# Attention: flipping two query tiles at a time, and taking the values two steps sooner

## The chip, the cores and the metric

One core of one Trainium2 chip. The core has a matrix engine (TensorE, "PE" in the profile, with its weight loads listed apart as "PEld"), a vector engine (DVE), an activation engine (ACT), a general engine (POOL) and a queue that issues transfers (SP). Each works through its own list of instructions in order; they wait for one another through semaphores. The metric is the device time of one execution in microseconds; the figure for a kernel is the median of its runs.

## The reference, cut to what matters

The program is one block of a network on 512 tokens of width 1024: a normalisation, one wide projection, a gated linear attention branch, a softmax attention branch, an output projection and a feed-forward part. The change sits in the softmax attention: 8 heads, 512 keys, the queries taken in four tiles of 128.

```python
def attend(qblk):
    s = jnp.einsum('bhqd,bhkd->bhqk', qblk, kt).astype(jnp.float32)
    p = jax.nn.softmax(s, axis=-1)
    return jnp.einsum('bhqk,bhkv->bhqv', p.astype(vt.dtype), vt)
```

After it come `merged = sigmoid(z_ma) * y_gla + sigmoid(z_mb) * y_mla` and `merged @ w_out`.

## The kernel before

All of it is float32 arithmetic built from three reduced-precision products: a matrix is split into a rounded part ("hi", a copy on ACT) and the remainder ("lo", a subtraction on DVE or POOL), and `mm3` (lines 88 to 90) issues hi·hi, hi·lo and lo·hi. So in the profile one product is three matmuls of the lines L88, L89 and L90, and one split is an ACT instruction of L93 and a DVE or POOL instruction of L94.

The attention is one loop over steps n; a step is one head and one query tile (tile number n = 4·head + query tile, 32 of them). What it issues for a tile:

- `att_scores`: three matmuls (L88 to L90, output `s`, 96 rows by 512 keys), a maximum on DVE (L1071, `top`), the exponential with the row sum on ACT (L1076, `e`).
- `att_normalise`, for two tiles at a time at an even step: a reciprocal on DVE (L1081), the even tile scaled on ACT (L1082), the odd tile scaled on DVE (L1083).
- `att_flip`: the tile's 128x512 probabilities are turned by four transposes on PE (L1091, output `tp`), then split out of PSUM: hi on ACT (L93, `pT`), lo on DVE (L94, `pT`). Two tiles fill the two halves of one pair of buffers `pT`.
- `att_values`, for two tiles: twelve matmuls (`av`, 256 columns, four blocks of keys by three products) that read the whole `pT` pair. L88 reads hi, L89 reads lo. After the second half of a head `merge` multiplies by the gate on DVE (L1119) and adds the other branch on POOL (L1122).

Between them the loop issues other work at fixed steps. At n mod 8 = 2, 3, 4 and 5 a "unit" makes the queries, keys and values of the next two heads (outputs `uq`, `uk`, `uv`: 9, 6, 12 and 12 matmuls) with the splits that belong to them; there are such units for heads 2 to 7, so they stop before step 24. At other steps weights are loaded and split for the output projection, which follows the loop (outputs `wox`, `wow`, `woz`).

In the kernel before, a tile is flipped three steps after its scores (`LAG_B`), one tile a step, and the values of a pair of tiles come six steps after the scores of its second tile (`LAG_C`; pair (0, 1) at n = 7). Written order in a step: normalisation, scores, unit, flip, loads and splits, values.

The written order is not the final one. The framework's planner takes the instructions of the whole program and lays down each engine's list, by priority and by what is ready; PSUM and SBUF buffers are handed out on the way. `s` and `tp` share four PSUM banks (tag "at"), the values and the units the other four (tag "mm"). Two helpers add constraints on the order alone, without a semaphore: `in_program_order` chains the instructions of an engine as written, and `goes_behind(late, early, engines)` puts the first instruction of one range behind the last of another. In the loop before, the maximum and exponential of step n stand behind the splits of the flip of step n - 2; PE's own order is free but for the first steps.

Of the kernel before, what the change touches and what calls it, by code (L numbers as in the profile page):

```python
# [26 lines left out]
MH, NOPE, ROPE, MV = 8, 64, 32, 128  # L27
# [29 lines left out]
def tile_block(ctx: ExitStack, tc: tile.TileContext, t, out: bass.AP):  # L57
# [13 lines left out]
    def u4(name, dt=F32R, shape=(P, 2, S)):  # L71
        return tl(list(shape), dt, "u4", 26, name)
# [4 lines left out]
    def ps(tag, name):  # L77
        serial[0] += 1
        return pp.tile([P, S], F32, tag=tag, bufs=4, name=f"{name}_{serial[0]}")
# [7 lines left out]
    def mm3(acc, lh, ll, rh, rl, start, stop, onto=False):  # L87
        nc.tensor.matmul(acc, lh, rh, start=start, stop=False, skip_group_check=onto)  # L88
        nc.tensor.matmul(acc, lh, rl, start=False, stop=False, skip_group_check=onto)  # L89
        nc.tensor.matmul(acc, ll, rh, start=False, stop=stop, skip_group_check=onto)  # L90

    def split(hi, lo, src, rest=nc.vector):
        nc.scalar.activation(hi, src, AF.Copy)  # L93
        rest.tensor_tensor(lo, src, raw(hi), op=ALU.subtract)  # L94
# [5 lines left out]
    def issued_after(ins, before):  # L100
        tc.add_manual_dep(
            ins, before,
            mybir.DependencyInfo(mybir.DependencyClass.NoSync, mybir.DependencyReason.DATA),
            reason="program order",
        )

    def traced():
        return len(nc.cur_bb.bb.instructions)

    def in_program_order(start, engines=None):  # L110

        prev = {}
        for ins in nc.cur_bb.bb.instructions[start:]:
            if engines is not None and ins.engine not in engines:
                continue
            before = prev.get(ins.engine)
            if before is not None:
                issued_after(ins, before)
            prev[ins.engine] = ins.name

    SP_ONLY = (mybir.EngineType.SP,)
    PE_ONLY = (mybir.EngineType.PE,)
    SPLITTERS = (mybir.EngineType.Activation, mybir.EngineType.DVE)

    def goes_behind(late, early, engines):

        ins = nc.cur_bb.bb.instructions
        for e in engines:
            a, b = [[i for i in ins[x:y] if i.engine == e] for x, y in (early, late)]
            if a and b:  # L130
                issued_after(b[0], a[-1].name)
# [932 lines left out]
    def att_scores(head, qt):  # L1064
        q, kb, _, _ = heads[head]
        tok = slice(qt * P, (qt + 1) * P)
        acc = ps("at", f"s{head}{qt}")
        d = slice(0, NOPE + ROPE)
        mm3(acc, q[d, 0, tok], q[d, 1, tok], kb[d, 0, :], kb[d, 1, :], True, True)
        top = sm("top", 1)  # L1070
        nc.vector.tensor_reduce(top, acc, axis=AX.X, op=ALU.max, negate=True)  # L1071
        e = u2(f"e{head}{qt}")
        if qt % 2 == 0:
            tots[head] = sm("tot", 2)
        tot = tots[head]
        nc.scalar.activation(e, acc, AF.Exp, bias=top, accum_out=tot[:, qt % 2 : qt % 2 + 1])  # L1076
        probs[head, qt] = e

    def att_normalise(head, qt):
        tot, a, b = tots[head], probs[head, qt], probs[head, qt + 1]  # L1080
        nc.vector.reciprocal(tot, tot)  # L1081
        nc.scalar.activation(a, a, AF.Copy, scale=tot[:, 0:1])  # L1082
        nc.vector.tensor_scalar(b, b, tot[:, 1:2], None, op0=ALU.mult)  # L1083

    def att_flip(head, qt):
        e = probs.pop((head, qt))
        if qt % 2 == 0:
            pTs[head, qt // 2] = [u4(f"pT{head}{qt}{x}", F32R, (P, NT, 256)) for x in range(2)]
        tp = ps("at", f"tp{head}{qt}")
        for k in range(NT):  # L1090
            nc.tensor.transpose(tp[:, k * P : (k + 1) * P], e[:, k * P : (k + 1) * P], ident)  # L1091
        hi, lo = pTs[head, qt // 2]
        c = slice((qt % 2) * P, (qt % 2 + 1) * P)
        split(hi[:, :, c], lo[:, :, c], tp.rearrange("p (k q) -> p k q", k=NT))

    def att_values(head, half):
        if half == 0:
            avs[head] = ps("mm", f"av{head}")
        acc = avs[head]
        hi, lo = pTs.pop((head, half))  # L1100
        _, _, vs, c = heads[head]
        for k in range(NT):
            vt = vs[k // 2]
            mm3(acc[:, half * 256 : (half + 1) * 256], vt[:, 0, k % 2, c], vt[:, 1, k % 2, c],
                hi[:, k, :], lo[:, k, :], k == 0, k == NT - 1)
        if head < MH - 1:
            if half == 1:
                merge(head, acc, (0, 1))
        else:
            merge(head, acc, (half,))  # L1110

    def merge(head, acc, halves_):

        p, c = head // 2, slice((head % 2) * HT, (head % 2 + 1) * HT)
        if p not in merged:
            merged[p] = u2(f"mx{p}"), u2(f"my{p}")
        y = g2[head]
        tok = slice(halves_[0] * HT, (halves_[-1] + 1) * HT)
        nc.vector.scalar_tensor_tensor(y[:, tok], y[:, tok], 1.0, acc[:, tok], op0=ALU.add, op1=ALU.mult)  # L1119
        for x in halves_:  # L1120
            t_ = slice(x * HT, (x + 1) * HT)
            nc.gpsimd.tensor_tensor(merged[p][x][:, c], y[:, t_], y1[head][:, t_], op=ALU.add)  # L1122
# [185 lines left out]
    in_program_order(fixed, SPLITTERS)  # L1308
    in_program_order(ordered, PE_ONLY)
    in_program_order(pooled, (mybir.EngineType.Pool,))  # L1310
    LAG_B, LAG_C = 3, 6
    units = up_units(1)
    at = traced()
    next(units)
    goes_behind((at, traced()), first_units, SPLITTERS[:1])
    attending = traced()
    sums_of, flipping, span = {}, {}, {}
    for n in range(4 * MH + LAG_C - 1):
        if n % 2 == 0 and 2 <= n <= 4 * MH:
            att_normalise((n - 2) // 4, (n - 2) % 4)  # L1320
        scored = traced()
        if n < 4 * MH:
            att_scores(n // 4, n % 4)
            if n - 2 in flipping:
                goes_behind((scored, traced()), flipping[n - 2], SPLITTERS)
        scored = scored, traced()
        if n == 0:
            goes_behind(scored, last_gate, PE_ONLY)
        if n == 3:
            span["fourth"] = scored  # L1330
        if 2 <= n % 8 < 7:
            at = traced()
            next(units, None)
            if n == 2:
                gla_turn(GH - 1)
            if n < 4:
                goes_behind((at, traced()), scored, PE_ONLY)
        if n in (6, 14):
            units = up_units(n // 8 + 2)
            at = traced()  # L1340
            next(units)
            if n == 6:
                goes_behind((at, traced()), span["fourth"], SPLITTERS[:1])
        b = n - LAG_B
        if 0 <= b < 4 * MH:
            flips = traced()
            att_flip(b // 4, b % 4)
            flipping[n] = flips, traced()

        if n == 20:  # L1350
            load_onto(B11, B12, w_out)
        extra = traced()
        for x, at in (("y", (18, 26, 34)), ("z", (20, 28, 36))):
            if n in at:
                p = at.index(n)
                to = (5, 6) if x == "y" else (7, 3)
                split_sum(wo_left[p], sums_of[p, x], *to, f"{x}o{p}", nc.gpsimd if p < 2 else nc.vector)
        if n in (19, 30):
            p = (19, 30).index(n)
            split_first(wo_left[p], merged[p][0], f"o{p}", nc.gpsimd)  # L1360
        if n < 4 * MH:
            goes_behind((extra, traced()), scored, SPLITTERS[:1])
        if n == 35:
            split_first(wo_left[2], merged[2][0], "o2")
        if n in (11, 13):
            streamed(1, B11, (n - 11) // 2)
            split_streamed(1, (n - 11) // 2)
        if n in (21, 23):
            streamed(2, B21, (n - 21) // 2)
        if n == 15:  # L1370
            load_w2(0, B11, w_out)
        if n == 17:
            at = traced()
            load_w2(0, B21, w_out, B22)
            span["sums"] = at, traced()
        if n == 23:
            load_onto(B21, B11, w_out)
        if n == 24:
            load_w2(0, B12, w_out)
            load_w2(0, B22, w_out)  # L1380
        c = n - LAG_C
        if c >= 0 and c % 2 == 1:
            att_values(c // 4, (c % 4) // 2)
        if n == 33:
            load_onto(B21, B12, w_out)
        if c > 0 and c % 8 == 7 and c // 8 < NP - 1:
            sums_of[c // 8, "y"], sums_of[c // 8, "z"] = merged_sums(c // 8, nc.gpsimd)
# [345 lines left out]
```

## Time and profile before

| | |
|---|---|
| median of three runs | 757.4 us (757.4 to 757.45) |
| the profiled execution | 757.7 us, of which the span of its instructions is 755.7 us |
| granted PE clock, mean | 0.999 |
| attention, from its first scores to its last values | 297.8 to 381.5 us of the span |
| exponentials, ACT | 32 of 689 ns |
| maxima, DVE | 32 of 682 ns |
| splits of flipped tiles, ACT and DVE | 32 of 597 ns and 32 of 682 ns |
| transposes of the attention, PE | 128 of 274 ns |

A row of a time line gives the start, the duration, the engine, the line, the operation, output <- inputs, shapes and how many instructions were merged; an idle time before the row stands in brackets with what ended it. Durations of matmuls overlap, because each is shown to the end of its pipeline: what a matmul costs in a stream is the distance from its start to the next start. The rows of a table of waits read "who waited <- for whom: us in total, times, longest". In a table of stretches each engine's busy time stands with its number of instructions, then the granted clock, the share of the transfer engines and GB/s.

### The profile page before, as it was taken

To read this page: it belongs to the slowest core of one execution; us is meant where nothing else is said; L and a number is where in the kernel's file an instruction comes from. 1 tells how busy PE (TensorE), PEld (TensorE's weight loads), DVE (VectorE), ACT (ScalarE), POOL (GpSimd) and SP (SyncE) were. 2 spreads that over 40 slices of the span, in tenths; PEclk is the share of its full clock that TensorE was granted. 3 is DMA by queue.
4 is the path that set the end of the run, shared out by engine and by line. 5 is a ranking of instruction groups with operands and counts; after the bars stand their busy time and mean duration, and the time that the engine had idled before them with its cause. 6 is when DMAs were issued, how large, how long until landed. Compare 5 with 4: busy or idle time off the path is not lost.

```text
span 755.7 us, 10257 instructions
## 1 busy us (share of the span) xinstructions
PE 746.8 (99%) x3720; PEld 632.8 (84%) x3720; DVE 586.5 (78%) x850; ACT 461.6 (61%) x780; POOL 165.3 (22%) x238
## 2 busy tenths in 40 slices
PE   9999999999999999999999999999999999999996
PEld 7888888888889888898888988888888888888885
DVE  7777887989787597898897787856696578748795
ACT  8456565686476575988865766345544555345644
POOL 0722110262662632136850100000000000000014
PEclk9999999999999999999999999999999999999999
DMA  9849582611321334228897421461126410650003
GB/s 315 256 125 230 177 174 82 113 29 29 83 57 31 47 86 114 73 84 198 264 201 227 129 57 56 140 194 57 56 65 204 122 57 4 206 153 0 29 1 111
DMA packets 94306, 87.59 MB, mean 116 GB/s; under 512 B 15696, under 2 KB 66896, under 8 KB 94256
## 3 DMA queue, kind: packets, MB, share of 16 engines
q1 hardware_dynamic: 87760, 74.33, 32.8%
q0 software_dynamic: 6208, 12.32, 9.3%
q8 instruction: 29, 0.48, 0.3%
q10 hardware_dynamic: 288, 0.28, 0.1%
q14 instruction: 21, 0.17, 0.1%
HBM read 83.25 MB, written 2.10 MB: 113 GB/s over the span
## 4 chain that ended last, share of the span: by engine, by line
PE 93%; DVE 3%; ACT 2%; DMA 1%; issue 1%; POOL 0%; POOLq 0%; ACTq 0%; SPq 0%
PE f L90 8%; PE f L88 8%; PE f L89 8%; PE gx L88 4%; PE gx L90 4%; PE gx L89 4%; PE first L330 3%; PE gz L90 2%; PE gz L88 2%; PE gz L89 2%; PE zb L88 1%; PE tp L1091 1%; PE zb L90 1%; PE zb L89 1%; PE wox L88 1%; PE wox L90 1%
## 5 line engine op out<-in xcount | busy, mean ns | idle before, releaser
L1672 POOL DMA_DIRECT2D gfin<-in_g_final x1 | 0.6, 628 | 284.1 <-PE f L90 284.1
L961 DVE TENSOR_TENSOR w<-w,w 128x1024 f32<-128x1024 f32 x32 | 38.7, 1221 | 0.3
L1071 DVE TENSOR_REDUCE top<-s 128x1 f32<-128x512 f32 x32 | 21.8, 682 | 2.9 <-PE s L90 2.6
L1076 ACT ACTIVATE e<-s,top 128x512 f32<-128x512 f32 x32 | 22.0, 689 | 2.7 <-DVE top L1071 2.4
L94 DVE TENSOR_TENSOR pT<-tp,pT 128x512 fp32r<-128x512 f32 x32 | 21.6, 682 | 2.4 <-ACT pT L93 2.2
L1399 DVE TENSOR_TENSOR h<-h,gx 128x512 f32<-128x512 f32 x32 | 21.5, 682 | 1.9 <-PE gx L90 1.8
L93 ACT ACTIVATE pT<-tp 128x512 fp32r<-128x512 f32 x32 | 18.9, 597 | 3.2 <-PE tp L1091 3.0
L1091 PE MATMUL tp<-ident,e 128*128 128x128 f32 x128 | 19.3, 274 | 0.4 <-ACT e L1082 0.2
L88 PE MATMUL av<-pT,v 128*128 128x256 f32 x64 | 18.9, 296 | 0.0
L93 ACT ACTIVATE ghb<-y 128x512 fp32r<-128x512 f32 x16 | 10.1, 633 | 14.0 <-DVE y L907 14.0
L1465 ACT ACTIVATE fa<-f 128x512 f32<-128x512 f32 x32 | 18.5, 578 | 0.0
L1091 PEld LDWEIGHTS tp<-ident,e 128*128 128x128 f32 x128 | 15.1, 140 | 3.9 <-ACT e L1082 0.8
L89 PE MATMUL av<-pT,v 128*128 128x256 f32 x64 | 18.2, 285 | 0.0
L90 PE MATMUL av<-pT,v 128*128 128x256 f32 x64 | 18.2, 285 | 0.0
L547 ACT ACTIVATE bds<-bd 128x512 f32<-128x512 f32 x4 | 2.4, 598 | 20.9 <-PE bd L543 20.9
L93 ACT ACTIVATE b_00h<-w 128x1024 fp32r<-128x1024 f32 x7 | 7.4, 1061 | 12.6 <-PE gz L90 6.0
L93 ACT ACTIVATE b_20h<-w 128x1024 fp32r<-128x1024 f32 x7 | 7.4, 1062 | 12.1 <-PE gz L90 6.0
L93 ACT ACTIVATE b_10h<-w 128x1024 fp32r<-128x1024 f32 x7 | 7.4, 1061 | 12.1 <-PE gz L90 6.0
L88 PE MATMUL s<-kbuf,q 96*128 96x512 f32 x32 | 14.2, 444 | 0.1
L1474 ACT ACTIVATE px<-fa 128x256 f32<-128x256 f32 x32 | 13.4, 418 | 1.0
L957 POOL DMA_DIRECT2D w<-in_w_out x10 | 12.3, 1401 | 6.5 <-DVE bo60l L94 5.3
L636 POOL DMA_DIRECT2D gvw<-in_w_in x4 | 4.8, 1226 | 38.7 <-DVE gvw L641 34.0
(1731 smaller groups left out, 2947.8 us busy)
## 6 DMA issues: line engine op xcount, KB each, us to landing
w<-in_w_ff SPq DMA_DIRECT2D x64, 256.0 KB, 3.4
w<-in_w_out POOLq DMA_DIRECT2D x10, 512.0 KB, 8.8
grw<-in_w_in SPq DMA_DIRECT2D x8, 512.0 KB, 9.3
zaw<-in_w_in SPq DMA_DIRECT2D x8, 512.0 KB, 7.9
gvw<-in_w_in SPq DMA_DIRECT2D x8, 512.0 KB, 4.5
w<-in_w_out SPq DMA_DIRECT2D x16, 256.0 KB, 5.9
x<-in_xt SPq DMA_DIRECT2D x8, 256.0 KB, 5.2
vw<-in_w_first SPq DMA_DIRECT2D x8, 256.0 KB, 5.4
```

The costliest lines, as they stand in the source:

```text
L88: nc.tensor.matmul(acc, lh, rh, start=start, stop=False, skip_group_check=onto)
L89: nc.tensor.matmul(acc, lh, rl, start=False, stop=False, skip_group_check=onto)
L90: nc.tensor.matmul(acc, ll, rh, start=False, stop=stop, skip_group_check=onto)
L93: nc.scalar.activation(hi, src, AF.Copy)
L94: rest.tensor_tensor(lo, src, raw(hi), op=ALU.subtract)
L330: nc.tensor.matmul(f_accs[i], a[:, i * P : (i + 1) * P], b, start=k == 0 and x == 0, stop=k == KD - 1 and x == 2)
L961: nc.vector.tensor_tensor(wq[dst][g], wq[x][g], wq[y][g], op=op)
L1071: nc.vector.tensor_reduce(top, acc, axis=AX.X, op=ALU.max, negate=True)
L1076: nc.scalar.activation(e, acc, AF.Exp, bias=top, accum_out=tot[:, qt % 2 : qt % 2 + 1])
L1091: nc.tensor.transpose(tp[:, k * P : (k + 1) * P], e[:, k * P : (k + 1) * P], ident)
L1399: nc.vector.tensor_tensor(hc, hc, acc, op=op)
L1465: nc.scalar.activation(a, acc, AF.Relu)
```

## The change

Three things in the loop. The flips: instead of one tile a step, both tiles of a pair are flipped at the odd step n (tiles n - 3 and n - 2), one directly behind the other, so that the odd tile comes one step sooner; their transposes are chained in written order on PE. The values: `LAG_C` goes from 6 to 4, so that pair (0, 1) is taken at n = 5, two steps after its flip, and `merge` and the sums that hang on it come two steps sooner. The order in an odd step: scores, unit, values of the pair flipped two steps ago, then the two flips; on PE the values stand behind that step's scores, and the flips behind the values. As `flipping` now has entries at odd steps alone, only odd steps have their maximum and exponential held behind the flips of two steps ago. The loop runs as many steps as before (37), and the last half of the last head is still taken after the loop.

```diff
-    LAG_B, LAG_C = 3, 6
+    LAG_B, LAG_C = 3, 4
...
-    for n in range(4 * MH + LAG_C - 1):
+    for n in range(4 * MH + LAG_C + 1):
...
-        b = n - LAG_B
-        if 0 <= b < 4 * MH:
+        c = n - LAG_C
+        if c >= 0 and c % 2 == 1 and c < 4 * MH - 1:
+            valued = traced()
+            att_values(c // 4, (c % 4) // 2)
+            goes_behind((valued, traced()), scored, PE_ONLY)
+        if n % 2 == 1 and LAG_B <= n <= 4 * MH + 1:
             flips = traced()
-            att_flip(b // 4, b % 4)
+            for b in (n - LAG_B, n - LAG_B + 1):
+                att_flip(b // 4, b % 4)
             flipping[n] = flips, traced()
+            in_program_order(flips, PE_ONLY)
+            if c > 0:
+                goes_behind(flipping[n], (valued, flips), PE_ONLY)
...
-        c = n - LAG_C
-        if c >= 0 and c % 2 == 1:
-            att_values(c // 4, (c % 4) // 2)
```

## The prediction, made before the changed kernel ran

> **What bounds the kernel now.** I read the page first, for the engine that sets the end.
>
> ```profile
> span 755.7 us, 10257 instructions
> PE 746.8 (99%) x3720; PEld 632.8 (84%) x3720; DVE 586.5 (78%) x850; ACT 461.6 (61%) x780; POOL 165.3 (22%) x238
> PE 93%; DVE 3%; ACT 2%; DMA 1%; issue 1%; POOL 0%; POOLq 0%; ACTq 0%; SPq 0%
> ```
>
> PE is busy for 99% of the span and is 93% of the chain that ended last. No matmul is added or removed by this change, so it can only act through time in which PE stands still. Next I asked for the waits of PE and of its weight loads within the attention, 296 to 384 us:
>
> ```profile
> PEld tp L1091 <- ACT e L1082: 0.8, 2, 0.7
> PEld tp L1091 <- issue: 0.6, 2, 0.3
> PEld s L88 <- ACT e L1076: 0.3, 1, 0.3
> PE tp L1091 <- ACT e L1082: 0.2, 1, 0.2
> ```
>
> That is all there is to win: 0.8 + 0.6 + 0.3 + 0.2 = 1.9 us. Of it 1.6 us stand before transposes, at two places above all, which the time line of PE shows:
>
> ```profile
> 359.13 0.39 PE L90 MATMUL s<-kbuf,q 96*128 96x512 f32 x1
> 359.75 0.66 PE L1091 MATMUL tp<-ident,e 128*128 128x128 f32 x4 [0.23 <-ACT e L1082]
> ...
> 363.98 0.28 PE L89 MATMUL av<-pT,v 128*128 128x256 f32 x1
> 364.39 0.63 PE L1091 MATMUL tp<-ident,e 128*128 128x128 f32 x4
> ```
>
> Both times the tile was not yet scaled by ACT (L1082). Both lie after step 24, where the units have ended and a pair of tiles has only its own work on PE. There a pair without a wait looks like this:
>
> ```profile
> 365.69 0.40 PE L88 MATMUL s<-kbuf,q 96*128 96x512 f32 x1
> ...
> 366.38 0.60 PE L1091 MATMUL tp<-ident,e 128*128 128x128 f32 x4
> 366.74 0.48 PE L88 MATMUL s<-kbuf,q 96*128 96x512 f32 x1
> ...
> 367.53 0.60 PE L1091 MATMUL tp<-ident,e 128*128 128x128 f32 x4
> 367.88 0.36 PE L88 MATMUL av<-pT,v 128*128 128x256 f32 x1
> 368.09 0.28 PE L89 MATMUL av<-pT,v 128*128 128x256 f32 x1
> ...
> 368.44 0.28 PE L89 MATMUL av<-pT,v 128*128 128x256 f32 x1
> ...
> 369.39 0.40 PE L88 MATMUL s<-kbuf,q 96*128 96x512 f32 x1
> ```
>
> Scores, flip, scores, flip, values: 369.39 - 365.69 = 3.70 us for the pair. Scores cost 366.38 - 365.69 = 0.69. A flip costs 0.44: from its start to the second matmul behind it 368.09 - 367.53 = 0.56, less the 0.12 that a values matmul takes in the stream (three from 368.09 to 368.44). Values cost what is left, 3.70 - 2 x 0.69 - 2 x 0.44 = 1.44.
>
> **The change, part by part: grouping the transposes.** Does a longer run of transposes cost less than two short ones? The kernel already has a run of eight:
>
> ```profile
> 375.43 0.39 PE L89 MATMUL wox<-bo10l,gao 128*128 128x512 f32 x1
> 375.66 1.03 PE L1091 MATMUL tp<-ident,e 128*128 128x128 f32 x8
> 376.45 0.36 PE L89 MATMUL av<-pT,v 128*128 128x256 f32 x1
> 376.65 0.28 PE L90 MATMUL av<-pT,v 128*128 128x256 f32 x1
> ```
>
> By the same reading 376.65 - 375.66 - 0.12 = 0.87, against 2 x 0.44 = 0.88. Sixteen times 0.01 is 0.2 us at most, within the rounding; I take 0. The change has no gain of its own on PE.
>
> A run of eight could also be dearer. The longest run of transposes before is sixteen:
>
> ```profile
> 423.45 1.91 PE L199 MATMUL mb<-ident,ms 128*128 128x128 f32 x16
> 423.00:426.00 3.00, 3.00 (x29) 3.00 (x28) 1.65 (x3) 1.70 (x4) 0.00 (x0) 1.00 0.50 147
> ```
>
> Over it the granted clock stays at 1.00, and it is twice as long as the new runs. [...]
>
> **The wait that goes.** At an odd step the new order on PE is scores, values, flip, flip. Between the last scores of a pair and its first flip PE now does two scores, two flips and two values blocks; before, it did two scores, two flips and one values block. That is 1.44 us more time for the scaling, against waits of 0.7 us at the longest. So I take all 1.6 us before transposes as gone; at the other bound none goes. The 0.3 us that scores waited for a bank stays.
>
> **The wait that comes.** Values of a pair now follow its flips at two steps' distance: flip, flip, scores, scores, values (and the units, where there are any). Before, three scores, three flips and a values block stood there. The splits of both tiles must be done first. What they take:
>
> ```profile
> 354.46 0.60 PE L1091 MATMUL tp<-ident,e 128*128 128x128 f32 x4
> 355.10 0.60 ACT L93 ACTIVATE pT<-tp 128x512 fp32r<-128x512 f32 x1 [0.23 <-PE tp L1091]
> 361.89 0.72 ACT L1082 ACTIVATE e<-e,tot 128x512 f32<-128x512 f32 x1 [0.23 <-DVE tot L1081]
> 362.52 1.08 ACT L93 ACTIVATE pT<-tp 128x512 fp32r<-128x512 f32 x2
> 363.56 1.28 DVE L94 TENSOR_TENSOR pT<-tp,pT 128x512 fp32r<-128x512 f32 x2
> 368.85 0.59 ACT L93 ACTIVATE pT<-tp 128x512 fp32r<-128x512 f32 x1
> 369.47 0.69 DVE L94 TENSOR_TENSOR pT<-tp,pT 128x512 fp32r<-128x512 f32 x1 [0.45 <-ACT pT L93]
> ```
>
> Count from the start of the second flip. ACT can begin a tile 355.10 - 354.46 = 0.64 after its flip started; the first tile's flip started 0.44 earlier, so its hi part starts at 0.20 and ends at 0.80. DVE follows 369.47 - 368.85 - 0.59 = 0.03 later, at 0.83, and two lo parts in a row take 1.28: both are done at 2.11. The second hi part, at 0.20 + 1.08 = 1.28, is not late. PE meanwhile ends the flip at 0.44 and two blocks of scores at 0.44 + 1.38 = 1.82; the first values matmul reads hi and may go, the second, at 1.94, reads lo and waits 0.17. A flip started after a wait is 0.06 longer (0.66 against 0.60), which I take for the refilling of the pipeline. So with ACT and DVE free at the right moment the wait is 0.23 us a pair: the lower bound.
>
> They are not free:
>
> ```profile
> 354.00:365.00 11.00, 10.64 (x73) 9.05 (x72) 10.28 (x20) 9.17 (x20) 8.34 (x10) 1.00 1.07 283
> 365.00:376.00 11.00, 11.00 (x83) 10.10 (x82) 9.47 (x19) 9.48 (x21) 7.60 (x9) 1.00 0.89 257
> ```
>
> (PE, PEld, DVE, ACT, POOL.) ACT is busy 83 to 86% and DVE 86 to 93% of these stretches. The scaling of the next pair by ACT becomes ready at about this moment, since the exponentials of the scores ahead of the values end while the values and flips run. It occupies ACT for 362.52 - 361.89 = 0.63. In front of the hi parts it makes the wait 0.23 + 0.63 = 0.86: the upper bound. Half of it is my value, 0.23 + 0.31 = 0.54, as an engine busy nine tenths of the time is met on average in the middle of an instruction.
>
> Other work can't shorten this within a pair. Values, flip, flip, split, values is now a ring: the flips stand behind the values by order, the values behind the splits by data. One turn is at least 1.44 + 0.88 + the 2.11 - 0.44 = 1.67 that the splits need after the flips, less the 0.12 of the one values matmul that needs no lo, and with 0.06 for the refilling 3.93 us, against 3.70 before. Behind the waiting values matmul stand the two flips and the next scores, and for these DVE's maxima and ACT's exponentials wait.
>
> How many pairs feel it? Where units lie between flip and values there are 1.4 us and more of cover. They don't at n = 7, 9, 15 and 17, nor at n = 23, 25, 27, 29, 31 and 33: ten of the sixteen. At the first four the planner can draw in the next unit, as it does now:
>
> ```profile
> 314.46 0.40 PE L88 MATMUL uq<-cqhl,wq2h 128*128 128x512 f32 x1
> 314.70 0.60 PE L1091 MATMUL tp<-ident,e 128*128 128x128 f32 x4
> 315.05 0.48 PE L89 MATMUL uq<-cqhl,wq2h 128*128 128x512 f32 x1
> ```
>
> I take 0.1 us each there (bounds 0 and 0.86), and the full 0.54 for the six late ones.
>
> **What else moves.** The merge of a head on DVE and POOL comes two steps sooner, and with it the sums for the output projection. On POOL's queue the merge of head 3 now stands ahead of the split of step 19 and that of head 4 ahead of the accumulating load of step 23. POOL has 2.7 us of 11 free in the stretches above, and no wait of PE names POOL, so I take 0; without that room a late load would show as a wait of `wox` or `wow`. On SP's queue nothing changes place. The `pT` buffers are held for two steps instead of four, so no transfer waits longer for one. After the loop PE has no wait listed before 384, and the last values are covered by output products as before: 0.
>
> **The sum.** Six times 0.54 is 3.2, four times 0.1 is 0.4, less 1.6: 2.0 us more. The profiled execution took 757.7 us with a span of 755.7; it would be 759.7, and the median, 0.3 us below it, 759.4. With the lower bound at the six, 6 x 0.23 - 1.6 = -0.2, 757.2; with the upper at all ten, 10 x 0.86 - 1.6 = 7.0, 764.4.
>
> **The rivals.**
>
> *A wash.* Either the splits are served promptly (0.23) and the old waits are merely exchanged for new ones, or the planner, which is bound to keep only values ahead of the two flips, slips the next scores between the two flips and so keeps the old spacing. For it: 0.23 is what free engines give. Against it: ACT and DVE are not free. About 757.2.
>
> *Faster.* The planner fills the six gaps with the first products of the output projection. Twelve of these (four rows by three matmuls), of 375.66 - 375.43 = 0.23 each, 2.8 us, are used now from 375 us on. With gaps of up to 2.8 / 6 = 0.46 us they would all be filled, and 1.6 to 1.9 us of waits vanish: 755.6. For it: the row at 375.43 shows such a product between values and flips. Against it: half of them need the merged pair of heads 2 and 3, the planner did not draw one into the gap at 359, and my gap is above 0.46.
>
> *Every exposed pair waits the full scaling,* in all ten places: 764.4. For it speaks that the planner takes what is ready first, and the scaling is ready first.
>
> *The clock.* If runs of eight transposes lost half the clock, 16 x 0.87 = 14 us: 771.4. [...]
>
> **How the numbers follow.** A measurement of this kernel can tell about 0.2%, 1.5 us, from no change: 755.9 to 758.9 is "same". Forecast (half a scaling in front, slower by 1.5 us or more) 0.50; every pair 0.10; the clock 0.02: slower 0.62. Wash 0.22. Faster 0.16, as 1.9 us is all there is and 1.5 of it would have to be gained net. The range goes from 756.0 to 764.0: it leaves out about 0.08 below, 0.05 of the dear case and the clock. The forecast's own range is 757.2 to 764.4.
>
> **What would show it.** Right: PE's waits in the attention change their name, from transposes waiting for the scaled tile (L1082) to `av` waiting for the lo part (L94, DVE) or the hi part (L93, ACT), most of them after step 22, 0.2 to 0.9 us each; runs of eight transposes cost 0.87. Wrong: no wait of `av` in the late part; scores that stand between the two flips; output products between the values of heads 6 and 7; a wait of `wox` on POOL; a granted clock under 1.00. The forecast fails as a whole if the listed waits of PE between 296 and 384 us sum to less than 2.

## The result, and the profile after

| | before | after |
|---|---|---|
| median | 757.42 us (757.40 to 757.75, 4 runs) | 764.77 us (764.69 to 765.73, 4 runs) |
| ratio | | 1.0097 (95%: 1.0085 to 1.0110) |
| span of the profiled execution | 755.7 us | 762.7 us |
| granted PE clock, mean | 0.999 | 0.998 |

The changed kernel is 7.35 us slower, 7.0 us on the span. The page after has the same matmuls, and the mean clock is the same to 0.001:

```profile
span 762.7 us, 10267 instructions
PE 749.0 (98%) x3720; PEld 632.7 (83%) x3720; DVE 586.5 (77%) x850; ACT 462.3 (61%) x780; POOL 165.3 (22%) x238
PE 91%; issue 3%; DVE 2%; ACT 1%; POOL 1%; DMA 0%; POOLq 0%; SPq 0%; DVEq 0%; ACTq 0%
```

DVE and ACT have hardly more to do than before (586.5 and 461.6 us then). PE stands still for longer, and the waits of its weight loads within the attention say before what:

```profile
PEld av L89 <- DVE pT L94: 6.4, 10, 1.0
PEld s L88 <- ACT e L1076: 2.0, 3, 0.7
PEld av L88 <- ACT pT L93: 1.8, 3, 1.0
PEld tp L1091 <- PE tp L1091: 0.2, 1, 0.2
```

The transposes no longer wait for a scaled tile. The values wait for their split tiles instead, ten times for a lo part, three times for a hi part, and the scores wait for a bank (an `s` that the exponential has not yet read). Weight loads run ahead of matmuls, so part of such a wait costs nothing: the matmuls themselves waited 3.6 us for the lo parts, 1.0 for the hi parts and 0.7 before scores. What it does cost is read from the distance of one pair's flips from the next pair's, on PE's time line of the late part:

```profile
356.14 1.03 PE L1091 MATMUL tp<-ident,e 128*128 128x128 f32 x8
...
360.76 1.26 PE L1091 MATMUL tp<-ident,e 128*128 128x128 f32 x8
...
365.60 1.04 PE L1091 MATMUL tp<-ident,e 128*128 128x128 f32 x8
...
368.26 0.38 PE L88 MATMUL av<-pT,v 128*128 128x256 f32 x1 [0.24 <-ACT pT L93]
...
369.31 0.39 PE L89 MATMUL av<-pT,v 128*128 128x256 f32 x1 [0.67 <-DVE pT L94]
...
370.72 1.04 PE L1091 MATMUL tp<-ident,e 128*128 128x128 f32 x8
...
371.83 0.39 PE L89 MATMUL s<-kbuf,q 96*128 96x512 f32 x1
...
373.96 0.39 PE L89 MATMUL av<-pT,v 128*128 128x256 f32 x1 [0.71 <-DVE pT L94]
...
375.38 1.03 PE L1091 MATMUL tp<-ident,e 128*128 128x128 f32 x8
...
377.33 0.50 PE L88 MATMUL s<-kbuf,q 96*128 96x512 f32 x1 [0.22 <-ACT e L1076]
...
378.58 0.38 PE L89 MATMUL av<-pT,v 128*128 128x256 f32 x1 [0.17 <-DVE pT L94]
...
379.99 1.09 PE L1091 MATMUL tp<-ident,e 128*128 128x128 f32 x8
381.82 0.39 PE L88 MATMUL av<-pT,v 128*128 128x256 f32 x1 [0.74 <-ACT pT L93]
```

Six pairs of flips are shown. A turn, from one of them to the next, holds the two flips, two blocks of scores and one of values, 3.70 us of PE's work. The five turns took 4.62, 4.84, 5.12, 4.66 and 4.61 us: 0.92, 1.14, 1.42, 0.96 and 0.91 too much, 5.35 together. Not all of it stands before values: in the first and the fifth turn about 0.5 stands before scores that waited for a bank (the row at 377.33; the first turn has one like it at 358.09), and 0.44 before the lo part (the row at 378.58). At the sixth place there are no scores left, and the values came 381.82 - 379.99 - 0.87 = 0.96 after the flip's end. That is 6.3 us for the six late places. The old waits of 1.6 us are gone, so the rest of the 7.0 is 7.0 + 1.6 - 6.3 = 2.3 us, in the earlier part. There the same time line has these idle times, one at each of the prediction's four early places (n = 7, 9, 15 and 17):

```profile
314.52 0.38 PE L89 MATMUL av<-pT,v 128*128 128x256 f32 x1 [0.55 <-DVE pT L94]
...
317.89 0.50 PE L88 MATMUL s<-kbuf,q 96*128 96x512 f32 x1 [0.22 <-ACT e L1076]
...
336.83 0.39 PE L89 MATMUL av<-pT,v 128*128 128x256 f32 x1 [0.45 <-DVE pT L94]
...
341.48 0.39 PE L89 MATMUL av<-pT,v 128*128 128x256 f32 x1 [0.24 <-DVE pT L94]
```

They sum to 1.46. An idle time is shown from the end of the last matmul's pipeline, and less than what was lost: at 378.58 it is 0.17, where the lo part's matmul came 0.33 later than it could (its hi part started at 378.13 and takes 0.12 in the stream), and the matmul behind it another 0.1 late. With some 0.2 more for each the four make about 2.3; this is an estimate.

What stood in front of the splits? DVE's time line for the turns from 365.60 and from 370.72:

```profile
367.37 0.69 DVE L1071 TENSOR_REDUCE top<-s 128x1 f32<-128x512 f32 x1 [0.30 <-PE s L90]
367.98 1.28 DVE L94 TENSOR_TENSOR pT<-tp,pT 128x512 fp32r<-128x512 f32 x2
...
370.92 0.69 DVE L1119 SCALAR_TENSOR_TENSOR tb<-tb,av 128x512 f32<-128x512 f32 x1 [1.06 <-PE av L90]
371.52 0.16 DVE L1081 RECIPROCAL tot<-tot 128x2 f32<-128x2 f32 x1
371.78 0.92 DVE L1083 TENSOR_SCALAR e<-e,tot 128x512 f32<-128x512 f32 x1
372.63 1.27 DVE L94 TENSOR_TENSOR pT<-tp,pT 128x512 fp32r<-128x512 f32 x2
```

POOL's, at the scaling of 0.92 us:

```profile
371.68 0.74 POOL L1122 TENSOR_TENSOR mx<-tb,yg 128x256 f32<-128x256 f32 x1 [0.85 <-DVE tot L1081]
```

and ACT's:

```profile
366.51 0.73 ACT L1082 ACTIVATE e<-e,tot 128x512 f32<-128x512 f32 x1 [0.23 <-DVE tot L1081]
367.14 1.07 ACT L93 ACTIVATE pT<-tp 128x512 fp32r<-128x512 f32 x2
...
371.35 1.08 ACT L93 ACTIVATE pT<-tp 128x512 fp32r<-128x512 f32 x2 [0.62 <-PE tp L1091]
```

In the first turn ACT's scaling holds the hi parts back until 367.14, and a maximum, which itself waited 0.30 us for the scores behind the flip, holds the lo parts back until 367.98; the second is done at 369.26 and its matmul starts at 369.31. In the second turn ACT was prompt, but on DVE the merge, the reciprocal and a scaling of 0.92 us (median 0.49 over the kernel) stand in front: the lo parts end at 373.90, the matmul starts at 373.96. The length of this scaling goes with POOL's part of the merge (L1122), which runs beside it: in the whole attention each of the seven scalings that took over 0.5 us ends 0.28 to 0.29 us after an instruction of POOL that runs beside it, here at 372.70 against 372.42. So the merge, which the change brings two steps sooner, stands in front of the lo parts on DVE, and the scaling behind it, beside POOL's part, takes 0.92; at the turn from 360.76 and at the last place it is the same (scalings of 0.92 and 0.98). That POOL's part is what lengthens the scaling is a reading of these rows: no run took that part away. It is not one scaling that is met halfway, but whatever the lists of the two engines hold.

### The profile page after: what moved, and what is told of

It reads as the page before. It is cut to its first block, busy times and chain, and to the rows that moved or that the text cites. A ratio compares the mean times of both kernels' runs of the same rounds, so it can differ in the third digit from the quotient of the medians.

```text
span 762.7 us, 10267 instructions
## 1 busy us (share of the span) xinstructions
PE 749.0 (98%) x3720; PEld 632.7 (83%) x3720; DVE 586.5 (77%) x850; ACT 462.3 (61%) x780; POOL 165.3 (22%) x238
## 4 chain that ended last, share of the span: by engine, by line
PE 91%; issue 3%; DVE 2%; ACT 1%; POOL 1%; DMA 0%; POOLq 0%; SPq 0%; DVEq 0%; ACTq 0%
PE f L89 8%; PE f L88 8%; PE f L90 8%; PE gx L88 4%; PE gx L89 4%; PE gx L90 4%; PE first L330 3%; PE gz L88 2%; PE gz L89 2%; PE gz L90 2%; PE zb L88 1%; PE zb L90 1%; PE zb L89 1%; DVE pT L94 1%; PE av L89 1%
## 5 line engine op out<-in xcount | busy, mean ns | idle before, releaser
L89 PEld LDWEIGHTS av<-pT,v 128*128 128x128 f32 x64 | 12.2, 190 | 6.6 <-DVE pT L94 6.4
L1091 PE MATMUL tp<-ident,e 128*128 128x128 f32 x128 | 16.8, 273 | 0.0
L88 PEld LDWEIGHTS av<-pT,v 128*128 128x128 f32 x64 | 12.1, 190 | 2.3 <-ACT pT L93 1.8
```

## The experiments

Times are compared with runs of the kernel before on the same chip; "+" is the difference of the medians.

| what runs | median, us | + | ratio (95%) |
|---|---|---|---|
| the change (after) | 764.77 | 7.35 | 1.0097 (1.0085 to 1.0110) |
| e1: flips in pairs, values at the old distance | 761.79 | 4.30 | 1.0055 (1.0040 to 1.0070) |
| e2: values two steps sooner, flips single | 761.47 | 3.98 | 1.0051 (1.0034 to 1.0068) |
| e7: values one step sooner, flips single | 759.48 | 1.60 | 1.0024 (1.0014 to 1.0033) |
| e3: after, flips ahead of values | 765.61 | 8.12 | 1.0107 (1.0092 to 1.0122) |
| e4: after, scalings behind the splits | 765.57 | 8.08 | 1.0104 (1.0089 to 1.0119) |
| e17: after, maxima and exponentials behind the splits | 765.90 | 8.10 | 1.0108 (1.0091 to 1.0125) |
| e5: after, no order fixed on PE | 762.38 | 4.50 | 1.0062 (1.0047 to 1.0077) |
| e6: e1, second lo part a step later | 759.97 | 2.09 | 1.0031 (1.0020 to 1.0042) |
| e10: after, second lo part a step later | 767.61 | 9.66 | 1.0132 (1.0118 to 1.0146) |
| e12: after, banks for the late scores | 765.54 | 7.59 | 1.0101 (1.0088 to 1.0115) |
| e11: after, no scalings | 761.88 | 3.93 | 1.0056 (1.0040 to 1.0070) |
| e13: after, no maxima | 762.22 | 4.61 | 1.0054 (1.0039 to 1.0069) |
| e14: after, neither | 765.97 | 8.36 | 1.0107 (1.0092 to 1.0121) |
| e16: e14, exponentials behind the splits | 763.74 | 5.94 | 1.0079 (1.0064 to 1.0094) |
| e9: before, maxima one step behind | 759.00 | 1.12 | 1.0015 (1.0006 to 1.0024) |
| e8: before, flips and values a step later | 759.19 | 1.24 | 1.0024 (1.0015 to 1.0033) |
| e15: e8, the last values one step sooner | 758.08 | 0.47 | 1.0007 (0.9998 to 1.0016) |

### The two halves of the change (e1, e2, e7)

e1 keeps the paired flips and gives the values their old distance:

```diff
-    LAG_B, LAG_C = 3, 4
+    LAG_B, LAG_C = 3, 6
...
-    for n in range(4 * MH + LAG_C + 1):
+    for n in range(4 * MH + 5):
```

> The flips stay paired and chained as in the changed kernel, but the values go back to six steps behind (four steps behind their flips). Theory A (a ring: flips stand behind values on PE, values behind the splits of flips only two steps older, and the splits behind other work on ACT and DVE): the 8.2 us of weight-load waits of av on pT fall under 1 us and the time is 757 to 758.5 us. Rival B (the pairing itself, which makes work for ACT and DVE arrive in bursts, costs the time): the waits stay above 5 us under some name and the time is 762 us or more.

Measured: +4.30. In its waits (weight loads, within the attention) the values are served, and the scores stand instead:

```profile
PEld s L88 <- ACT e L1076: 4.1, 7, 1.0
PEld av L88 <- ACT pT L93: 0.8, 1, 0.8
```

So pairing has a price of its own, which the prediction had at nothing. The reading of these waits is that two splits in a row stand on ACT and DVE, that the maxima and exponentials behind them come later, and the banks of `s` with them; e6 tests it below.

e2 is the other half, the kernel before with the values two steps sooner (the same edit of `LAG_C` in before, the last half still taken after the loop):

```diff
-    LAG_B, LAG_C = 3, 6
+    LAG_B, LAG_C = 3, 4
```

> The kernel before with the values two steps sooner and nothing else: one flip a step, PE's order left to the planner. Theory A: without the order that holds the flips behind the values there is no ring, the planner lays flips and scores into the gap, 757.5 to 760 us. Rival (the shorter distance alone, whatever the order of the flips, costs the time): 763 us or more.

Measured: +3.98, with waits of both kinds:

```profile
PEld av L88 <- ACT pT L93: 1.8, 3, 0.9
PEld tp L1091 <- ACT e L1082: 1.8, 2, 1.3
PEld av L89 <- DVE pT L94: 1.5, 4, 0.5
```

Single flips still wait for their scaling here; only the order "values ahead of flips" of the change removes that. e7 is the same with `LAG_C = 5`:

> The kernel before with the values one step sooner instead of two (757.5 with none, 761.5 us with two). If the distance from split to values decides, with one step (some 1.1 us of scores and a flip) less cover: the waits of av appear in the tight places only, 758 to 760 us. If what costs is the odd step itself, in which values meet scaling and maxima, the values in even steps cost nothing or more than two steps: 757.5 or 762 us.

Measured: +1.60. Six, five and four steps: 0, +1.60, +3.98. Each step that is taken from the distance costs; that the second costs more than the first is not clear of the spread of these runs. Pairing alone (+4.30) and distance alone (+3.98) sum to 8.3, against 7.35 for both.

### The order on PE (e3, e5)

e3 turns the order round: scores, flips, values.

```diff
-            valued = traced()
-            att_values(c // 4, (c % 4) // 2)
-            goes_behind((valued, traced()), scored, PE_ONLY)
...
+            goes_behind(flipping[n], scored, PE_ONLY)
+        if c >= 0 and c % 2 == 1 and c < 4 * MH - 1:
+            valued = traced()
+            att_values(c // 4, (c % 4) // 2)
+            goes_behind((valued, traced()), flipping[n], PE_ONLY)
```

> The changed kernel with the two order constraints exchanged: in each odd step scores, then the two flips, then the values of the older pair. The values get two flips (0.87 us) more of cover and nothing stands behind them in a ring. Theory A: the waits of av, about 1 us each now, shrink to 0.1 to 0.3, and the flips wait for the scaling again by up to 1.6 us in all as before the change: 757.5 to 760 us. Rival C (the maxima, held behind the splits on DVE, starve ACT, whatever the order of flips and values): 762 us or more.

Measured: +8.12. The waits change their name and not their size:

```profile
PEld tp L1091 <- ACT e L1082: 7.6, 5, 2.0
```

With the values behind them the flips meet the unscaled tile again. (This profile is of the longest of the four runs, 767.12 us, in which the clock was 0.50 from 320.4 to 323.8 us; the others took 764.92 to 765.71.) In e5 PE's constraints on flips and values are taken out and the planner chooses:

```diff
-            goes_behind((valued, traced()), scored, PE_ONLY)
...
-            in_program_order(flips, PE_ONLY)
-            if c > 0:
-                goes_behind(flipping[n], (valued, flips), PE_ONLY)
```

> The changed kernel without its new order on PE: the flips no longer stand behind the values nor in a chain, the values no longer behind the scores of their step; distances as in the changed kernel. Theory A (the ring by order): the planner separates flips and values as it can, most of the loss goes, 757.5 to 760 us. Theory D (the distances alone crowd ACT and DVE, whatever the order on PE): 763 to 766 us, and the waits are still those of av on pT and of scores on exponentials.

Measured: +4.50; `av` waits 2.5 + 1.9 us, `s` 1.7, `tp` 0.9. The fixed order is worth 7.35 - 4.50 = 2.85 us of the loss. The rest stays without it; it is the price of the shorter distance and the pairing, which e1 and e2 show each alone.

### Moving work on ACT and DVE (e4, e17)

e4 leaves the scalings in and puts them behind the splits of the last flip:

```diff
+            scaling = traced()
             att_normalise((n - 2) // 4, (n - 2) % 4)
+            if n - 1 in flipping:
+                goes_behind((scaling, traced()), flipping[n - 1], SPLITTERS)
```

> The changed kernel with one constraint more: the reciprocal and the two scalings of a pair stand behind the splits of the flips of the step before, on ACT and on DVE. Theory A with the prediction's term (one scaling in front of the splits): the waits fall towards the bound for free engines, 0.23 us in about ten places, 2 to 3 us in all, and the time is 758.5 to 761 us. Rival C (the maxima and exponentials are late, and the scalings only fill the hole they leave): 763 to 766 us, since the exponentials and what hangs on them are not earlier.

Measured: +8.08, `av` still waits 5.2 + 2.2 us. Its five late turns take 4.02, 5.26, 5.13, 4.03 and 4.63 us, 0.8 less in all than the change's. The clock takes this back: in every run of e4 the mean granted clock was 0.995, and in its profile it was 0.57 over the four us from 316.0, behind 1.5 us in which PE was busy for 0.46. That is as much as 3.4 us at half clock, and loses 1.7 us. Without that spell e4 would be at about +6.4, an estimate: 1 us better than the change, where leaving the scalings out (e11) gains 3.4. e17 does the same with maxima and exponentials:

```diff
+            if n - 1 in flipping:
+                goes_behind((scored, traced()), flipping[n - 1], SPLITTERS)
```

> The changed kernel, whole, with the same constraint: maxima and exponentials of an even step stand behind the splits of the flips of the step before, on DVE and ACT. If maxima that wait for their scores ahead of the splits are a good part of the loss: 761.5 to 763.5 us. If the scalings ahead of the splits and the late exponentials make nearly all of it: 764 to 766 us.

Measured: +8.10:

```profile
PEld av L89 <- DVE pT L94: 6.5, 9, 1.0
PEld s L88 <- ACT e L1076: 2.6, 4, 0.7
PEld av L88 <- ACT pT L93: 2.0, 2, 1.4
```

As measured, neither gains on the change. A likely reason, not shown turn by turn, is that what is put behind the splits of this turn is what the next turn's flips or scores need: the lists must hold it somewhere, and PE asks for it soon.

### The second lo part, a step later (e6, e10)

These take the split of the pair's second tile out of `att_flip` and issue it after the next step's scores, its lo part behind their maximum. e6 does so at the old distance (on e1), e10 at the new one (on after):

```diff
-    def att_flip(head, qt):
+    def att_flip(head, qt, later=False):
...
+        if later:
+            return lambda: split(hi[:, :, c], lo[:, :, c], tp.rearrange("p (k q) -> p k q", k=NT))
...
+        if n - 1 in flipping:
+            at = traced()
+            second()
+            goes_behind((at, traced()), scored, SPLITTERS[1:])
```

> Paired flips with the values at the old distance (the first experiment, 761.8 us, where scores wait 4.1 us for the exponentials that free their bank), but the split of the second tile of a pair is issued behind the next step's scores, its lo part behind their maximum. Theory C (with two splits in a row ahead of it on DVE the maximum comes late, the exponential with it, and the bank): ACT's waits for the maximum fall from 9.4 us towards the 2.4 us of the kernel before, the waits of scores under 2 us, 757.5 to 760 us. Rival (paired transposes cost through something else, such as holding two banks at once): 761 us or more.

> The changed kernel (values two steps sooner, flips paired), with the split of a pair's second tile issued behind the next step's scores and its lo part behind their maximum on DVE. Theory A (the direct ring: flip, split, values): the second lo part comes one maximum, 0.6 us, later and values wait for it, so 0.6 us more in about nine places, 768 to 771 us. Theory C (late maxima and exponentials hold the ring): 760 to 763 us.

Measured: e6 +2.09, half of e1's 4.30; e10 +9.66, 2.3 above after, with these waits:

```profile
PEld av L89 <- DVE pT L94: 9.0, 10, 1.5
PEld av L88 <- ACT pT L93: 4.6, 8, 1.6
```

With distance to spare the split is better behind the maximum, without it worse. It is the same instruction; what decides is which of its neighbours has slack. This is the most direct sign in the runs that in the changed kernel the splits of every pair set PE's pace.

### Banks (e12)

The odd scores of heads 6 and 7 get banks of the other four:

```diff
-        acc = ps("at", f"s{head}{qt}")
+        acc = ps("mm" if head >= 6 and qt % 2 else "at", f"s{head}{qt}")
```

> The changed kernel with the scores of every second tile of heads 6 and 7 in the other four PSUM banks, which the units have left by then. If banks are part of the cost: the two late waits of scores for an exponential (1.3 us with their refilling) go, and scores can run ahead, 760.5 to 763.5 us. If not: 764 to 765.5 us, the waits moving to the values behind them.

Measured: +7.59, no gain; the profiled execution has after's span of 762.7. The late scores do get their banks and run ahead, and the values wait in their place:

```profile
PEld av L89 <- DVE pT L94: 5.2, 9, 0.9
PEld av L88 <- ACT pT L93: 4.3, 6, 1.1
```

The late turns take 4.66, 4.80, 5.11, 4.65 and 4.63 us, within 0.04 of after's, though PE now has nine matmuls of scores to do in the first of them and three in the fifth. So what PE has to do in a turn does not set its length, and neither do the banks: the round from flips through the splits to the values does.

### Leaving work out (e11, e13, e14, e16)

e11 leaves out the two scalings of a pair (L1082, L1083):

```diff
-        nc.scalar.activation(a, a, AF.Copy, scale=tot[:, 0:1])
-        nc.vector.tensor_scalar(b, b, tot[:, 1:2], None, op0=ALU.mult)
```

> The changed kernel with the two scalings of a pair left out (the reciprocal stays, the probabilities go on without their row's factor), which takes 0.63 us from ACT and 0.5 to 0.9 us from DVE per pair, and the link from the exponentials to the flips. Theory D (work crowded into the time between flips and values on ACT and DVE): the waits of av fall from 8.2 to 2 to 3 us, 757.5 to 760.5 us. Theory A in its bare form (the ring is flip, split, values alone, with engines free): no change, 763 to 766 us.

Measured: +3.93, so the scalings are worth 3.4 us of the 7.35. What stays is seen on DVE and on PE at one of its long waits:

```profile
365.47 0.69 DVE L1071 TENSOR_REDUCE top<-s 128x1 f32<-128x512 f32 x1 [0.91 <-PE s L90]
366.08 1.28 DVE L94 TENSOR_TENSOR pT<-tp,pT 128x512 fp32r<-128x512 f32 x2
```

```profile
367.42 0.39 PE L89 MATMUL av<-pT,v 128*128 128x256 f32 x1 [1.18 <-DVE pT L94]
```

DVE stood idle for 0.91 us with the lo parts behind it in its list, because the maximum at the head of the list waited for scores. e13 leaves out the maxima in place of the scalings:

```diff
-        nc.vector.tensor_reduce(top, acc, axis=AX.X, op=ALU.max, negate=True)
...
-        nc.scalar.activation(e, acc, AF.Exp, bias=top, accum_out=tot[:, qt % 2 : qt % 2 + 1])
+        nc.scalar.activation(e, acc, AF.Exp, scale=0.05, accum_out=tot[:, qt % 2 : qt % 2 + 1])
```

> The changed kernel without the row maxima: the exponential is taken of the scores times 0.05, with no maximum subtracted. That takes 0.6 us a tile from DVE, and the wait of ACT for it; scalings and splits stay. If the maxima on DVE, with the late exponentials, hold the splits of the flips and the banks of the scores: the 2.0 us of waits of scores go and those of av fall, 759 to 761.5 us. If the scalings alone stand in front of the splits: 763 to 765 us.

Measured: +4.61, so the maxima are worth 2.7 us. In three of the four runs the granted clock was 0.995 or 0.996; the one run at 0.998 took 760.93 us, 3.3 above the kernel before. Without the clock's part the maxima would thus be worth about 4.0, from a single run. e14 leaves out both:

> The changed kernel without maxima (as the run beside it) and without the two scalings of a pair. What is left between flips and values is the two splits, so the bound for free engines should show: about 0.24 us of waiting in each of some eight places and the last place, which has no scores ahead of it, 1 us. Against the kernel before with its 1.6 us of old waits gone that is about 1 us slower at most, 757.5 to 759.5 us. If it stays above 761 us, something beside ACT's and DVE's queues costs the time.

Measured: +8.36, a miss. Four of the five late places that have scores are at the floor, 0.23 to 0.25 us, as the theory has it, and the last place costs 0.90. But at two places PE stood for 2.0 and 2.9 us. The first is the fifth of those late places, behind the scores at 368.98: an exponential that waited for its scores had come to the head of ACT's list, ahead of the hi parts:

```profile
368.78 0.60 ACT L1074 ACTIVATE e<-s 128x512 f32<-128x512 f32 x1 [2.71 <-PE s L90]
369.37 1.08 ACT L93 ACTIVATE pT<-tp 128x512 fp32r<-128x512 f32 x2
```

The second is an early place. There no exponential but the split of a weight stood ahead of the hi parts, and waited for its transfer:

```profile
313.45 1.06 ACT L93 ACTIVATE bo11h<-bo11f 128x1024 fp32r<-128x1024 f32 x1 [1.22 <-DMA bo11f<-in_w_out]
```

The late stand was followed by a spell at half the clock, from 371.2 us (columns as in the prediction; the clock is the third figure from the right):

```profile
371.20:374.70 3.50, 3.37 (x16) 3.37 (x17) 0.86 (x3) 0.34 (x2) 1.18 (x1) 0.51 0.63 114
```

The mean granted clock of this profile is 0.993, against 0.998 for the change. This spell takes 1.7 of 764.7 us, 0.002; what is left would fit a second one behind the early stand, an estimate.

e16 is e14 with the exponentials put behind the splits by the same constraint as in e17:

> The run without maxima and scalings (766.0 us; five late places waited 0.23 to 0.26 us, two places 2 to 3 us behind an exponential that stood ahead of the splits on ACT and itself waited for its scores), with one constraint more: the exponentials of an even step stand behind the splits of the flips of the step before. If the order in ACT's queue is what made the two long waits: every place waits about 0.24 us, the last 1.1, the granted clock stays at 1.00, 758 to 760 us. If the long waits stay or move: 762 us or more.

Measured: +5.94. The late part is now what the prediction called the floor; PE's time line:

```profile
364.12 1.04 PE L1087 MATMUL tp<-ident,e 128*128 128x128 f32 x8
...
368.14 1.03 PE L1087 MATMUL tp<-ident,e 128*128 128x128 f32 x8
```

A turn takes 4.02 us (3.93 was worked out), the waits in all five late turns are 0.24, the last place costs 0.91, and the time is still no better than e1's. The early place of e14 spoils it, which the constraint does not touch. On ACT the same split of a weight stood ahead of the hi parts and waited for its transfer:

```profile
313.23 1.06 ACT L93 ACTIVATE bo11h<-bo11f 128x1024 fp32r<-128x1024 f32 x1 [1.14 <-DMA bo11f<-in_w_out]
314.19 1.06 ACT L93 ACTIVATE pT<-tp 128x512 fp32r<-128x512 f32 x2
```

PE stood for 1.3 and 1.1 us, and then ran 6.8 us at half clock, of which 3.4 are lost. Its span of 762.6 less 2.4 and 3.4 would be 756.8, against 755.7 for the kernel before: an estimate, since these two stretches were not taken out by a run.

### From the other side (e9, e8, e15)

If too little distance is the cause, is the kernel before short of it too, and would another order on ACT and DVE help it? e9 keeps before's flips and values, and holds each maximum and exponential behind the splits of the last step in place of the one before that (`n - 1` for `n - 2`):

> The kernel before with one constraint moved: maximum and exponential of a step stand behind the splits of the flip of the step before, instead of two steps before. Flips and values unchanged. Theory C (maxima held behind the newest splits on DVE are what the pairing costs): scores and transposes begin to wait for exponentials and scalings, 2 to 5 us slower, 759.5 to 762.5 us. Rival: the planner has this order already or there is slack enough, 757 to 758 us.

Measured: +1.12: no gain. e8 gives before one step more for flips and values (`LAG_B, LAG_C = 4, 7`):

> The kernel before with flips and values both one step later (four and seven steps behind the scores; values then fall on even steps), one flip a step. It gives the scaling one step more and leaves the distance from split to values as before. If distance is what matters: the 1.6 us of waits before transposes go and nothing comes, 755.8 to 757 us, faster than both. If the even step or the buffers held longer cost something: 757.5 to 760 us.

Measured: +1.24. Its attention waits only 1.2 us, but the last values end a step later, with the merge after them in the open:

```profile
PE av L88 <- DVE tb L1119: 1.9, 1, 1.9
```

e15 is e8 with the last pair within the loop taken a step sooner (`c = 29` at `n == 35`):

> The kernel before with flips and values one step later, but the values of the first half of head 7 at step 35 as before. In the run with everything later (759.2 us) the waits of the attention were 1.2 us, but the last values waited 1.9 us for the merge of that half, which stood behind other splits on DVE. If that is all: 756.5 to 757.6 us, at or just under the kernel before. If the wait only moves: 758.5 to 760 us.

Measured: +0.47, an interval that includes no difference. More distance than the kernel before has gains nothing here: of the 1.6 us that it could win, the tail takes back as much. No version beat the kernel before.

## Why the prediction went right and wrong

The sign was right, and so was the new place of the waits: `av` on the lo and the hi part, most after step 22. The size was not: 2.0 us were forecast on the span, 7.0 came, and 764.77 lies above the range. Point by point:

- *The old waits of 1.6 us go.* Right: 0.2 us of waits before transposes are left.
- *Grouping costs nothing on PE.* Right for PE: the flip from 370.72 to the second matmul behind it at 371.83, less the 0.23 that a scores matmul takes, is 0.88, against 0.87 from the old run of eight. Wrong for the engines behind: e1 shows +4.30 for flips in pairs at the old distance. The prediction did not price two pairs of splits in a row on ACT and DVE at all.
- *The clock.* The changed kernel has runs of eight all through its attention, and the clock there is 1.00 (the row is the stretch with those at 365.60 and 370.72). No run shows the term behind 771.4, half the clock over eight transposes in a row; what the runs showed in its place is 1.00.

```profile
365.00:376.00 11.00, 9.38 (x65) 8.06 (x64) 7.54 (x14) 8.00 (x18) 6.40 (x8) 1.00 0.97 232
```

- *The floor of 0.23 us and the ring of 3.93.* Right as a mechanism: with nothing in front of the splits e16 has 0.24 and 4.02.
- *Half a scaling in front, 0.54 at the six late places, 0.86 at most.* **This is the step that failed.** The places were right, the term was mis-sized: measured 0.92, 1.14, 1.42, 0.96, 0.91 and 0.96, each above even its upper bound, 6.3 us where 3.2 was put. (In the first and the fifth about half stands before scores; e12 gives those scores banks, the turns stay as long, and the values wait instead.) The argument was that an engine busy nine tenths of the time is met in the middle of one instruction. But the engines work through a list in order: in e14 ACT was idle for 2.71 us ahead of the exponential at 368.78, with the hi parts behind it, whose transposes had ended at 367.99; in e11 DVE was idle until the maximum at 365.47, with the lo parts behind it, whose hi parts had run on ACT from 364.34 to 365.42. What matters is the whole of what the list holds ahead of the split: on DVE a merge, a reciprocal and a scaling that took 0.92 instead of 0.49, or a maximum that itself waits for scores issued behind the flip, and on ACT the scaling. e11 and e13 price them: 3.4 us for the scalings, 2.7 for the maxima, or about 4.0 by the one run that kept its clock. With both left out and the splits first (e16) the five turns are at 4.02.
- *0.1 us each at the four early places.* Too little: some 2.3 us, by difference. The rows at 314.52, 336.83 and 341.48 show waits of a lo part there too, and that at 317.89 a wait of scores.
- *The merge two steps sooner: 0.* Wrong: on DVE it stands in front of the lo parts, and the scaling that runs beside POOL's part of it takes 0.92 to 0.98. No run prices the merge alone; its 0.6 and the 0.43 on the scaling are read from the rows.
- *The scores' wait for a bank stays at 0.3.* Wrong: 2.0 us in three waits. But taking two of them away (e12) gains nothing, since the values then wait for as long.
- *The last place.* The place at n = 33 was priced like the others, but no scores are left there for cover; it cost 0.96. After it the planner did put products of the output projection behind the first values matmul, and nothing more was lost.
- *The rivals.* "Every exposed pair waits the full scaling", 764.4, comes nearest in time, though it is not what happened: the places do not wait for one scaling on ACT but for unequal sums on both engines. That its time is so near is chance. The wash needed free engines or scores between the flips, and the faster case output products in the six gaps; they came at the last one alone.

What stays open: why moving work (e4, e17) does not help was not taken apart turn by turn; the split of the early 2.3 us over its places rests on a reading of idle times; and where the granted clock is lower in most runs (0.992 to 0.996 in e4, e13, e14 and e16), the difference of the median is not the price of the edit alone.

## What to carry to other kernels

Where one engine's output comes back to it through two engines with lists in order, the distance is not to be priced by what the round trip takes when they are free (0.24 us a turn in e16), nor by half an instruction (0.54; 0.91 to 1.42 were measured): write down every instruction that their lists hold between, ask for each what it waits for, and add them. Grouping work on the engine that sets the end can make the same work arrive in lumps at the engines behind it, and these then delay what the first engine needs next (e1: +4.30). If a distance of six steps has no visible waits, a shorter one is not free: here two steps cost 4.0 us and the first alone 1.6. And ask of each instruction in those lists what runs beside it: here a scaling that took 0.47 to 0.49 us alone took up to 1.38 where POOL worked beside it.

## What the runs showed of the hardware that was not expected

Short stands of PE were followed by spells at half the clock. In e14 one matmul stood between two idle times of 1.13 and 0.45 us, and the clock was 0.50 for the next 3.4 us, which costs 1.7 us, nearly as much again as the stand of 2.0; in e16 it was 0.50 for 6.8 us, from 316.1 to 322.9, at the second of two idle times of 1.27 and 1.10 us with one matmul between them; in e4 PE was idle for 0.33 us between 312.0 and 314.5 and for 1.04 between 314.5 and 316.0, with the clock at 1.00, which then was 0.57 over the next 4.0. Stands of 0.7 us in the changed kernel (the rows at 369.31 and 373.96) did nothing of the kind: the clock was 1.00 from 365 to 376. The length of one stand alone does not decide: in e3 an idle time of 1.55 us, up to 320.38, was followed by 3.4 us at 0.50, while behind one of 1.18 us in e11 (the row at 367.42) and one of 1.08 in e10 (up to 366.32) the values matmuls came 0.12 us apart, where they came 0.21 apart in e14's spell. What decides it, no run here tested.

DVE's scaling of one tile (L1083) took from 0.47 to 1.38 us for one and the same shape in the changed kernel, and from 0.47 to 1.42 in the kernel before. In the changed kernel it goes with what POOL does: the seven that took 0.55 us or more each ran beside a TENSOR_TENSOR of POOL and ended 0.28 to 0.29 us after it. Eight ran beside none and took 0.47 to 0.49; one, at 379.10, began 0.30 us ahead of one of POOL's and took 0.48.
